# Early gate weights, one background list and early residuals in a one-core streaming-encoder layer

## Chip, cores and metric

The kernel runs on one core of a Trainium2 chip. The metric is the device time of one execution in microseconds: the median of three runs is 1506.96 us (1506.39 to 1509.68). The engines are named as in the profile: PE (TensorE, matrix products), DVE (VectorE), ACT (ScalarE), POOL (GpSimd) and SP (SyncE, which issues most loads).

## What is computed

One layer on 1024 tokens of width 1024, in float32. A first half mixes tokens in three branches, each with a sigmoid gate; a second half is a gated feed-forward network of width 2816.

```
n = rmsnorm(h);  proj = n @ w_in            # pool input, q, k, v, xq, 3 x 1024 gate columns
y_pool = pool_mixer(pool input) @ w_pool_o  # trailing means over 2, 4, 8, 16 tokens, 4 groups
y_sb   = stick_breaking(q, k, v) @ w_sb_o   # 8 heads, strictly causal
y_x    = cross_attention(xq, mem) @ w_x_o   # 4 heads, 256 memory tokens, softmax
merged = sum of sigmoid(gate_b) * y_b
h = h + rmsnorm(merged @ w_out)
gu = rmsnorm(h) @ w_ffn_in
h = h + rmsnorm((silu(gu[:, :2816]) * gu[:, 2816:]) @ w_ffn_out)
```

## The kernel before

**Products.** Tiles are 128 rows by 512 columns (C). Each float32 product is three fp32r matmuls (`mm3`, L167 to L171): every operand is split into a rounded part and the rest. A weight tile is loaded into `ws` (3 buffers) or `b2` (8 buffers), ACT casts it to `wh` and DVE subtracts to `wl` (5 buffers each; `split`, L163 and L164, for `ws`; `parts`, L250 and L251, for any tile). PSUM has eight banks: `pa` 3, `pz` 2, `pt` 2, `pv` 1.

**Strassen-like pairs.** Most projections go by `pairs` (L444): for two weight columns, four quarters of the weights (`quarters`, loads into four `b2` tiles) and seven products of half depth, of 4 x 3 matmuls of 512 columns each, instead of eight. The first two of the seven are `opening` (L434): bank `X` holds product 11, bank `Y` product 12, and L440 adds the copy of the first to the second. Then come S1 and S2, whose weights are differences made on DVE (L456, L460), then S4, S3 and 22. The activations' sums for S1 to S4 are made and split on DVE and ACT too (L516 to L537). The next job's opening is put between S3 and 22 of this one; the first call opens two jobs at its start.

**The order of the first half.** Pooling products and norms; products of the memory tokens; then three early gate tiles of branch 1 for the first half of the tokens (`early`, L510, weights by `split`), with the operand sums; then the first `pairs` call (xq, q 0, q 2), the keys (k 0, k 2), the values (seven products written out, L700 to L770), four gate pairs (branch 0, m = 0, 2, 4, 6), and the attention. The remaining gate tiles of branches 1 and 2 are the list `later` (L804): single products of 12 matmuls, which `fill(n)` puts between the attention's units.

**Background.** Small steps run at the `aside()` places: three in each job of `pairs`, one behind each of the first six products of the values. Sixteen are units of the cross-attention (`recall`, L624: scores L584 and L585, softmax L586 to L597, four transposes L604, products L615 and L616); they are put on the list after the first `pairs` call. They read `xq` back from DRAM, and SP issues these reads in program order. What is left after the values runs in a loop (L771). Then `w_mix` is split, and eight pooling steps (`pooled`, L646) and the first `fetch` of the attention's operands go on the list for the gate pairs.

**Attention.** `units` are 32 (head pair, pair of 128-token rows, head). `sticks` (L833) makes scores, sigmoids and running products on PE, ACT, POOL and DVE one unit ahead; `values` (L872) transposes (L881), splits on ACT and DVE (L174, L175) and multiplies with v (L893, L896). Before each unit's values stand as many fillers as its share of the work, four before the first, eight kept for the end.

**The end.** After the two halves of the merged product and the feed-forward network, the last product (22) is made tile by tile, four tiles of 128 rows; behind each, `finish` (L1265) loads the two residual halves (`load`, L115, on SP), squares (L1276), multiplies with the gain (L1279), takes the power on POOL (L180), multiplies and adds the residual (L1285) and writes half on SP and half on ACT (L1286). `load` keeps SP's order as the program is written; for the rest a scheduler sets each engine's order ahead of time from the program's order and a simulated time line.

Of the kernel before, what the change touches and what calls it, by code (L numbers as in the profile page):

```python
# [9 lines left out]
F32R = mybir.dt.float32r  # L10
# [4 lines left out]
P = 128  # L15
# [13 lines left out]
LEAD = 8  # L29
HOLD = 3  # L30
EARLY = 3
FILL_FIRST = 4
FILL_LAST = 8
TB = C // P
# [4 lines left out]
def hybrid_block(  # L39
# [77 lines left out]
    def ps_a():  # L117
        return pa.tile([P, C], F32, tag="pa", name="pa")
# [160 lines left out]
    for c in range(NC):  # L279
        rb = t_r()[:, :C]  # L280
        rms_rows(ssum[c], C, pc[:, c * TB : (c + 1) * TB], rb)
        rbc.append(rb)
        pool_step(4 + c)
        if c == 1:
            first_mk = [split(w_mk[0, half]) for half in range(2)]
        else:
            for q in range(HK):
                a11.append(normed_x(q, 0, t_c()[:, :C]))
                A["11"][q] = parts(a11[q], t_act(), t_act())
# [141 lines left out]
            load(raw[h][i], src[m + i, h])  # L431
        return raw

    def opening(raw, sink):  # L434
        (b11, b12), (b21, b22) = raw
        X, Y = ps_a(), ps_a()
        product(X, w_parts(b11), "11", True)
        p1 = copied(X)
        product(Y, w_parts(b21), "12", True)
        nc.vector.tensor_add(p1, Y, p1)  # L440
        sink(0, 0, p1)
        return X

    def pairs(jobs, raws=None):  # L444
# [1 line left out]
        raws = raws or [jobs[0][0]()]  # L446
        ahead = len(raws)

        opened = [opening(raws[j], jobs[j][1]) for j in range(ahead)]
        for j, (_, sink) in enumerate(jobs):  # L450
            (b11, b12), (b21, b22) = raws[j]
            if len(raws) == j + 1 < len(jobs):
# [56 lines left out]

    def early(m):  # L510
        for half in range(2):
            gate_step(KT + m, half, 0, split(w_gate[KT + m, half]))


    early(0)
# [130 lines left out]
    def pooled(g, c):  # L646
# [38 lines left out]
                nc.gpsimd.dma_start(d, t)  # L685
        return step

    pairs(
        [(lambda: quarters(w_xq, 0), to_parts(xq_d, 0))]
        + [(lambda m=m: quarters(w_q, m), to_parts(q_d, m)) for m in (0, 2)],  # L690
        xq_raws,
    )
    background += [recall(n) for n in range(len(units))]
    pairs([(lambda m=m: quarters(w_k, m), to_parts(k_d, m)) for m in (0, 2)])


    v_d = [
        [dram.tile([P, C], F32R, name=f"v{j}{h}") for h in range(2)] for j in range(KT)
    ]
    v_sb = [[None, None] for _ in range(KT)]  # L700
    W = C // 2
    raw = [[[None, None], [None, None]], [[None, None], [None, None]]]
    for h, i in ((0, 0), (1, 0), (0, 1), (1, 1)):
# [64 lines left out]
    sub2(b21, b21, b11)  # L768
    v_product(X, two(b21), "22")
    to_values(1, 0, X)  # L770
    while background:  # L771
        aside()


    heads = {}

    def fetch(p, c):

        if c == 0:
            heads[p] = [[[None] * NC for _ in range(2)] for _ in range(3)]  # L780
        qst, kh, kl = heads[p]
        for e in range(2):
            for tiles in (qst, kh, kl):
                tiles[e][c] = t_c(F32R)[:, :C]
            stacked(qst[e][c], q_d[p][c], e)
            twice(kl[e][c], k_d[p][c][1], e)
            twice(kh[e][c], k_d[p][c][0], e)
        if p % 2 == 0 and c == 1:
            for j in range(KT - 1, -1, -1):
                v = v_sb[j][p // 2] = t_a(F32R)  # L790
                load(v, v_d[j][p // 2])

    mix_h, mix_l = split(w_mix)
    background += [pooled(g, c) for g in range(4) for c in (1, 0)] + [lambda: fetch(0, 0)]
    pairs([(lambda m=m: quarters(w_gate, m), to_gate(0, m)) for m in range(0, KT, 2)])
    for q in range(HK):
        u = normed_x(q, 1, t_d()[:, :C])
        A["21"][q] = parts(u, t_act(), t_act())
# [4 lines left out]

    later = [  # L804
        (b * KT + m, half, c)
        for b in (1, 2)
        for m in range(KT)
        for half in range(2)
        for c in range(1 if b == 1 and m < EARLY else 0, NC)
    ]  # L810
# [451 lines left out]
        g_post[1][h] = t_r()[:, :C]  # L1262
        load(g_post[1][h], post[1:2, h * C : (h + 1) * C].broadcast_to([P, C]))

    def finish(t, first_ps):  # L1265

        st = small.tile([P, 8], F32, tag="st1", name="st1")
        res = []
        for h in range(2):
            u = t_b2()  # L1270
            load(u, hid_d[t][h])
            res.append(u)
        for h in (1, 0):
            src = first_ps if h == 0 and first_ps is not None else y[t][h]
            sq = t_d()[:, :C]
            nc.scalar.activation(sq, src, AF.Square, scale=1.0 / 32, accum_out=st[:, h : h + 1])  # L1276
            if src is not y[t][h]:
                y[t][h] = t_c()[:, :C]
            nc.vector.tensor_mul(y[t][h], src, g_post[1][h])  # L1279
        v = small.tile([P, 4], F32, tag="rv", name="rv")  # L1280
        nc.vector.tensor_scalar(v[:, 0:1], st[:, 0:1], st[:, 1:2], EPS, ALU.add, ALU.add)  # L1281
        r = inv_root(v, 1)
        for h in range(2):
            o = y[t][h]
            nc.vector.scalar_tensor_tensor(o, o, r[:, 0:1], res[h], ALU.mult, ALU.add)  # L1285
            (nc.gpsimd if t < TB else (nc.sync, nc.scalar)[h]).dma_start(  # L1286
                out[t, :, h * C : (h + 1) * C], o
            )
# [4 lines left out]
    for k in range(HF):  # L1293
# [2 lines left out]
        room = [t_act() if k < 8 else t_a(F32R) for _ in range(4)]  # L1296
        last.append((parts(u, *room[:2]), parts(b_of("T4", k), *room[2:])))
        if k < TB:
            finish(k, None)
    for i in range(TB):  # L1300
        add_bank(s5[i], X[i])
        y[TB + i][1] = s5[i]
    for i in range(TB):
        bs = slice(i * P, (i + 1) * P)
        for k in range(HF):
            (ah, al), (wh, wl) = last[k]
            mm3(X[i], ah[:, bs], al[:, bs], wh, wl, False, k == HF - 1, True)
        finish(TB + i, X[i])


# [76 lines left out]
```

## Time and profile before

| | |
|---|---|
| median of three runs | 1506.96 us (1506.39 to 1509.68) |
| profiled execution | 1507.43 us |
| its span, first to last instruction | 1505.7 us |
| mean granted TensorE clock | 0.988 |
| busy: PE, DVE, ACT, POOL | 96%, 69%, 47%, 22% |
| early gates and first openings | 60 to 110 us |
| last cross-attention units | 257 to 274 us |
| gate pairs | from 274 us |
| attention | 410 to 640 us |
| last tile's end | 1491 to 1505.7 us |

A matmul counts as busy from its start to its modelled end, and the next one starts before that; so a busy PE may still lose time, and the granted clock has to be read beside it. The span leaves out 1.7 us of the profiled execution's time. The table's stages are the stretches of the program in the order above; the rows below give each its idle time, its clock and its waits.

### The profile page before, as it was taken

Reading aid. Unit: us, or ns where it says so; the run is one execution under the profiler, and the core shown is the slowest. Engines: PE = TensorE matmul, PEld = TensorE weight load, DVE = VectorE, ACT = ScalarE, POOL = GpSimd, SP = SyncE. Lnnn points to the kernel's source line nnn. Section 1 sums busy time; section 2 is a strip of 40 time slices with the busy share of each in tenths; the row PEclk is TensorE's granted clock in tenths of the full one; section 3 lists DMA queues with packets and bytes.
Section 4 is the critical chain, followed back from the end, with each engine's and each line's share of the span. In section 5 each row is a group of like instructions: output and inputs, shape, how many; then the busy total and the mean of one; then the engine's idle time right before and its main releaser. Section 6 shows DMA issues by size and latency. Waiting matters only on the chain.

```text
span 1505.7 us, 20998 instructions
## 1 busy us (share of the span) xinstructions
PE 1449.7 (96%) x6914; PEld 1203.1 (80%) x6914; DVE 1037.0 (69%) x1732; ACT 706.1 (47%) x1405; POOL 330.6 (22%) x612
## 2 busy tenths in 40 slices
PE   9989999999999999899999999999999999999996
PEld 8768898777887888778887777888888887888875
DVE  8795777794879878745514597765566666478475
ACT  8554556553656656522235673233333333434452
POOL 0201212122244332354445310000011112000011
PEclk9999999999999999999999999999999999999998
DMA  8726446458322531475555454443465656754354
GB/s 277 221 96 183 140 127 189 151 184 274 109 96 84 164 122 59 147 232 187 154 161 193 145 180 152 152 130 127 140 195 191 195 175 212 233 184 147 108 151 161
DMA packets 126222, 245.77 MB, mean 163 GB/s; under 512 B 16656, under 2 KB 20256, under 8 KB 126112
## 3 DMA queue, kind: packets, MB, share of 16 engines
q1 hardware_dynamic: 97952, 173.09, 37.5%
q0 software_dynamic: 27584, 70.29, 13.4%
q8 instruction: 54, 0.88, 0.3%
q10 hardware_dynamic: 576, 1.05, 0.2%
q14 instruction: 56, 0.46, 0.1%
HBM read 174.11 MB, written 69.73 MB: 162 GB/s over the span
## 4 chain that ended last, share of the span: by engine, by line
PE 77%; DVE 7%; DMA 6%; issue 5%; ACT 2%; POOL 2%; SPq 1%; POOLq 0%; ACTq 0%; DVEq 0%
PE pa L169 16%; PE pa L170 15%; PE pa L171 15%; PE pz L171 5%; PE pz L170 5%; PE pz L169 5%; PE pt L171 3%; PE pt L169 3%; PE pt L170 3%; DMA ws<-in_w_gate_dram 2%; PE pt L881 1%; SPq L115 1%; DMA d<-in_x_dram 1%; PE pv L893 1%; PE pv L896 1%
## 5 line engine op out<-in xcount | busy, mean ns | idle before, releaser
L169 PE MATMUL pa<-act,wh 128*128 128x512 f32 (+1 forms) x572 | 226.5, 396 | 10.7 <-ACT wh L163 4.6
L171 PE MATMUL pa<-act,wl 128*128 128x512 f32 (+1 forms) x572 | 223.5, 394 | 1.3 <-DVE wl L251 1.3
L170 PE MATMUL pa<-act,wh 128*128 128x512 f32 (+1 forms) x572 | 224.1, 392 | 0.0
L250 ACT CAST wh<-b 128x512 fp32r<-128x512 f32 x159 | 97.9, 622 | 162.7 <-PE pa L170 100.2
L169 PEld LDWEIGHTS pa<-act,wh 128*128 128x128 f32 x572 | 109.1, 191 | 35.5 <-ACT wh L163 5.0
L251 DVE TENSOR_TENSOR wl<-b,wh 128x512 fp32r<-128x512 f32 x159 | 108.1, 685 | 36.4 <-ACT wh L250 23.6
L163 ACT CAST wh<-ws 128x512 fp32r<-128x512 f32 (+1 forms) x121 | 73.9, 612 | 120.0 <-PE pa L170 34.8
L171 PEld LDWEIGHTS pa<-act,wl 128*128 128x128 f32 x572 | 108.4, 190 | 24.2 <-DVE wl L251 2.2
L170 PEld LDWEIGHTS pa<-act,wh 128*128 128x128 f32 x572 | 109.2, 191 | 20.8
L250 ACT CAST wh<-ws 128x512 fp32r<-128x512 f32 x76 | 47.5, 625 | 105.9 <-DVE ws L1153 42.5
L164 POOL TENSOR_TENSOR wl<-ws,wh 128x512 fp32r<-128x512 f32 x52 | 67.8, 1311 | 78.0 <-ACT wh L163 78.0
L250 ACT CAST d<-b 128x512 fp32r<-128x512 f32 x66 | 40.7, 620 | 93.1 <-PE pt L170 46.0
L169 PE MATMUL pa<-a,wh 128*128 128x512 f32 x200 | 78.9, 397 | 4.0 <-ACT wh L250 1.7
L164 DVE TENSOR_TENSOR wl<-ws,wh 128x512 fp32r<-128x512 f32 (+1 forms) x69 | 46.1, 672 | 52.1 <-ACT wh L163 32.6
L251 DVE TENSOR_TENSOR d<-b,d 128x512 fp32r<-128x512 f32 x66 | 45.3, 689 | 52.8 <-ACT d L250 51.7
L171 PE MATMUL pa<-a,wl 128*128 128x512 f32 x200 | 78.2, 393 | 0.0
L170 PE MATMUL pa<-b,wh 128*128 128x512 f32 x196 | 76.5, 391 | 0.0
L175 DVE TENSOR_TENSOR d<-pt,d 128x512 fp32r<-128x512 f32 (+1 forms) x96 | 60.8, 637 | 16.7 <-ACT d L174 16.2
L1119 POOL DMA_DIRECT2D ff<-c x44 | 23.8, 540 | 215.2 <-DVE c L1174 123.6
L174 ACT CAST d<-pt 128x512 fp32r<-128x512 f32 (+1 forms) x96 | 52.7, 557 | 29.3 <-PE pt L881 15.1
L180 POOL TENSOR_TENSOR rc<-rv,mhalf 128x1 f32<-128x1 f32 (+2 forms) x15 | 14.3, 956 | 230.9 <-DVE rv L1281 199.0
L862 DVE TENSOR_TENSOR_SCAN r<-a,zero 128x512 f32<-128x512 f32 (+1 forms) x64 | 53.4, 842 | 15.4 <-POOL a L850 14.6
(419 smaller groups left out, 4043.0 us busy)
## 6 DMA issues: line engine op xcount, KB each, us to landing
b<-in_w_ffn_in_dram SPq DMA_DIRECT2D x88, 256.0 KB, 2.7
d<-gt SPq DMA_DIRECT2D x48, 256.0 KB, 2.9
ws<-in_w_ffn_in_dram SPq DMA_DIRECT2D x44, 256.0 KB, 2.8
ff<-c POOLq DMA_DIRECT2D x44, 256.0 KB, 3.1
b<-ffS SPq DMA_DIRECT2D x44, 256.0 KB, 2.6
ws<-in_w_gate_dram SPq DMA_DIRECT2D x38, 256.0 KB, 3.6
gt<-g POOLq DMA_DIRECT2D x36, 256.0 KB, 2.5
b<-ff SPq DMA_DIRECT2D x33, 256.0 KB, 3.6
```

The source lines that it names most:

```text
L115: tc.keep_in_program_order(queue.dma_start(dst, src))
L163: nc.scalar.copy(wh[:, :n], ws[:, :n])
L164: lo.tensor_sub(wl[:, :n], ws[:, :n], wh[:, :n].bitcast(F32))
L169: nc.tensor.matmul(ps, lh, rh, start=first, stop=False, skip_group_check=onto)
L170: nc.tensor.matmul(ps, lh, rl, start=False, stop=False, skip_group_check=onto)
L171: nc.tensor.matmul(ps, ll, rh, start=False, stop=last, skip_group_check=onto)
L174: nc.scalar.copy(hi, ps)
L175: nc.vector.tensor_sub(lo, ps, hi.bitcast(F32))
L250: nc.scalar.copy(hi, src)
L251: eng.tensor_sub(lo, src, hi.bitcast(F32))
L862: nc.vector.tensor_tensor_scan(ex[:, lo + 1 : C + 1], rest[:, lo:], zero.broadcast_to([P, C - lo]), start, ALU.mult, ALU.add,)
L1119: nc.gpsimd.dma_start(ff_d[n][k], t)
```

## The change

Five edits. The first gate tile's weights are loaded into the two `g` tiles while the first memory weights are loaded, and `early(0)` splits them from there. The second of the two openings of the first `pairs` call takes its `Y` from `pz`. The pairs of branch 0 cover m = 0 to 5 (`PAIRED`), and m = 6, 7 go to the head of `later`. All units of the cross-attention, the eight pooling steps and the first `fetch` are one list, filled when the weights of q 2 are loaded (at the second job of the first call); the loop that empties it stands behind the gate pairs, and `w_mix` is split before the first `pairs` call. In `finish` the loads of the residuals become `residual`, which for the last four tiles is called before the last product.

```
+PAIRED = 6
...
         if c == 1:
             first_mk = [split(w_mk[0, half]) for half in range(2)]
+            first_gate = [t_g(), t_g()]
+            for half in range(2):
+                load(first_gate[half], w_gate[KT, half])
...
-    def opening(raw, sink):
+    def opening(raw, sink, other=ps_a):
         (b11, b12), (b21, b22) = raw
-        X, Y = ps_a(), ps_a()
+        X, Y = ps_a(), other()
...
-        opened = [opening(raws[j], jobs[j][1]) for j in range(ahead)]
+        opened = [opening(raws[j], jobs[j][1], (ps_a, ps_z)[j]) for j in range(ahead)]
...
     def early(m):
         for half in range(2):
-            gate_step(KT + m, half, 0, split(w_gate[KT + m, half]))
+            w = w_parts(first_gate[half]) if m == 0 else split(w_gate[KT + m, half])
+            gate_step(KT + m, half, 0, w)
...
-    pairs(
-        [(lambda: quarters(w_xq, 0), to_parts(xq_d, 0))]
-        + [(lambda m=m: quarters(w_q, m), to_parts(q_d, m)) for m in (0, 2)],
-        xq_raws,
-    )
-    background += [recall(n) for n in range(len(units))]
...
+    mix_h, mix_l = split(w_mix)
...
+    def second_q():
+        background.extend(recall(n) for n in range(len(units)))
+        background.extend(pooled(g, c) for g in range(4) for c in (1, 0))
+        background.append(lambda: fetch(0, 0))
+        return quarters(w_q, 2)
+
+    pairs(
+        [
+            (None, to_parts(xq_d, 0)),
+            (None, to_parts(q_d, 0)),
+            (second_q, to_parts(q_d, 2)),
+        ],
+        xq_raws,
+    )
...
+    pairs([(lambda m=m: quarters(w_gate, m), to_gate(0, m)) for m in range(0, PAIRED, 2)])
     while background:
         aside()
...
-    mix_h, mix_l = split(w_mix)
-    background += [pooled(g, c) for g in range(4) for c in (1, 0)] + [lambda: fetch(0, 0)]
-    pairs([(lambda m=m: quarters(w_gate, m), to_gate(0, m)) for m in range(0, KT, 2)])
...
-        for b in (1, 2)
-        for m in range(KT)
+        for b in range(3)
+        for m in range(PAIRED if b == 0 else 0, KT)
...
+    def residual(t):
+        res = [t_b2(), t_b2()]
+        for h in range(2):
+            load(res[h], hid_d[t][h])
+        return res
+
+    def finish(t, first_ps, res):
...
+    res = [residual(TB + i) for i in range(TB)]
     for i in range(TB):
...
-        finish(TB + i, X[i])
+        finish(TB + i, X[i], res[i])
```

DVE's order around the first job's S2 is, before (a row is line, operation, output from inputs; `b_1039` to `b_1045` are the four weight quarters of xq; L440 is the addition of the second job's opening):

```order
L251 TENSOR_TENSOR a<-c,a 128x512
L251 TENSOR_TENSOR b_1200<-r,b_1199 128x512
L251 TENSOR_TENSOR d<-c,d 128x512
L460 TENSOR_TENSOR b_1039<-b_1045,b_1039 128x512
L471 TENSOR_TENSOR b_1041<-b_1041,b_1039 128x512
L440 TENSOR_TENSOR c<-pa,c 128x512
L251 TENSOR_TENSOR wl<-b_1039,wh 128x512
```

And now, where L440, L460 and L251 have become L444, L464 and L252:

```order
L444 TENSOR_TENSOR c<-pz,c 128x512
L252 TENSOR_TENSOR a<-c,a 128x512
L252 TENSOR_TENSOR b_1195<-d,b_1194 128x512
L471 TENSOR_TENSOR b_1091<-b_1093,b_1091 128x512
L252 TENSOR_TENSOR d<-c,d 128x512
L252 TENSOR_TENSOR a<-c,a 128x512
L464 TENSOR_TENSOR b_1039<-b_1045,b_1039 128x512
```

The second opening's addition, now from `pz`, has moved six operations ahead of the difference for S2; the difference itself stands one instruction later, counted from the engine's start.

PE's order between the values and the gate pairs is, before (L615 and L616 are the products of a cross-attention unit, L604 its transposes, L584 and L585 the scores of the next):

```order
L171 MATMUL pa<-act,wl 128x512
L615 MATMUL pv<-d,c 128x256
L616 MATMUL pv<-d,c 128x256
L615 MATMUL pv<-d,c 128x256
L616 MATMUL pv<-d,c 128x256
L604 MATMUL pt<-ident,c 128x128 x6
L584 MATMUL pz<-c,r 128x256
L585 MATMUL pz<-c,r 128x256
L604 MATMUL pt<-ident,c 128x128 x2
```

And now, behind the last product of the values (`mm3` is L170 to L172; products into `pv` are those of a pooling step):

```order
L170 MATMUL pa<-act,wh 128x512
L171 MATMUL pa<-act,wh 128x512
L170 MATMUL pv<-d,wh 128x512
L172 MATMUL pa<-act,wl 128x512
L171 MATMUL pv<-d,wh 128x512
L172 MATMUL pv<-d,wl 128x512
L170 MATMUL pa<-a,wh 128x512
L171 MATMUL pa<-a,wh 128x512
```

The cross-attention's small products have left this place, and gate products with a pooling step between them stand there.

PE's order at the end of the attention is, before (L881 transposes, L893 and L896 multiply with v):

```order
L881 MATMUL pt<-ident,b_7318 128x128
L881 MATMUL pt<-ident,b_7329 128x128
L881 MATMUL pt<-ident,b_7318 128x128
L893 MATMUL pv<-d,a 128x256
L896 MATMUL pv<-d,a 128x256
L893 MATMUL pv<-d,a 128x128
L896 MATMUL pv<-d,a 128x128
```

And now, with the products with v in L905 and L908:

```order
L170 MATMUL pa<-act,wh 128x512
L171 MATMUL pa<-act,wh 128x512
L172 MATMUL pa<-act,wl 128x512
L170 MATMUL pa<-act,wh 128x512
L905 MATMUL pv<-d,a 128x256
L908 MATMUL pv<-d,a 128x256
L905 MATMUL pv<-d,a 128x128
L908 MATMUL pv<-d,a 128x128
```

Gate products have moved between the transposes and the products with v of one of the last units.

## Rows read from the trace of the kernel before

**Rows 1.** The page, part 1: busy us (share of the span) xinstructions of each engine.

```profile
PE 1449.7 (96%) x6914; PEld 1203.1 (80%) x6914; DVE 1037.0 (69%) x1732; ACT 706.1 (47%) x1405; POOL 330.6 (22%) x612
```

**Rows 2.** Stretches: from:to, length; busy us by engine; PE clock, DMA share, GB/s.

```profile
60.00:80.00 20.00, 15.40 (x86) 13.34 (x85) 18.11 (x34) 9.57 (x19) 4.70 (x9) 0.91 1.02 315
80.00:110.00 30.00, 25.20 (x102) 19.52 (x101) 29.96 (x51) 16.55 (x30) 2.70 (x5) 0.94 0.14 43
257.00:274.00 17.00, 12.81 (x55) 10.15 (x55) 13.20 (x37) 9.24 (x26) 2.21 (x5) 0.80 0.46 133
274.00:344.00 70.00, 69.45 (x300) 56.43 (x300) 61.56 (x113) 37.55 (x65) 16.66 (x31) 0.98 0.57 181
410.00:640.00 230.00, 217.76 (x1217) 184.61 (x1215) 187.52 (x294) 140.85 (x317) 81.79 (x217) 0.98 0.36 114
620.00:640.00 20.00, 15.97 (x100) 13.55 (x98) 15.53 (x30) 13.02 (x32) 7.87 (x17) 0.90 0.59 197
655.00:820.00 165.00, 165.00 (x726) 135.80 (x725) 73.13 (x99) 48.21 (x96) 84.51 (x73) 1.00 0.54 169
```

**Rows 3.** Time lines of the end: start us, us, engine, instruction, [idle before <-releaser].

```profile
1491.27 0.39 PE L171 MATMUL pv<-a 128*128 128x512 f32 x1
...
1484.05 0.60 ACT L1276 ACTIVATE d<-pa 128x512 f32<-128x512 f32 x1 [8.24 <-PE pa L171]
...
1491.69 0.60 ACT L1276 ACTIVATE d<-pv 128x512 f32<-128x512 f32 x1 [3.00 <-PE pv L171]
...
1477.52 0.68 DVE L251 TENSOR_TENSOR a<-a 128x512 fp32r<-128x512 f32 x1
...
1486.82 1.41 DVE L1285 SCALAR_TENSOR_TENSOR c<-c,rc,b 128x512 f32<-128x512 f32 x2
...
1500.66 0.75 DVE L1285 SCALAR_TENSOR_TENSOR c<-c,rc,b 128x512 f32<-128x512 f32 x1 [3.21 <-DMA b<-hid]
1501.90 0.75 DVE L1285 SCALAR_TENSOR_TENSOR c<-c,rc,b 128x512 f32<-128x512 f32 x1 [0.49 <-DMA b<-hid]
...
1497.24 0.87 SPq L115 DMA_DIRECT2D b<-hid  x2
```

**Rows 4.** Waits of PE, 250 to 276 us: line, releaser: us, times, longest.

```profile
PE pv L615 <- DVE d L175: 1.9, 1, 1.9
...
PE pa L169 <- ACT c L417: 0.3, 1, 0.3
```

**Rows 5.** Waits of PE, whole span: the one on the read of `xq`.

```profile
PE pz L584 <- DMA r<-xq: 0.8, 1, 0.8
```

**Rows 6.** Time line of SP's queue, 46 to 190 us.

```profile
57.11 2.42 SPq L115 DMA_DIRECT2D ws<-in_w_gate_dram  x2
59.57 3.09 SPq L115 DMA_DIRECT2D d<-in_x_dram  x6
...
141.49 38.78 SPq L115 DMA_DIRECT2D r<-xq  x8
```

**Rows 7.** Waits of PE, 46 to 112 us.

```profile
PE pa L169 <- ACT wh L163: 4.6, 1, 4.6
PE pa L169 <- DVE c L440: 2.9, 1, 2.9
PE pa L169 <- ACT wh L250: 1.7, 1, 1.7
```

**Rows 8.** Time line of DVE, 60 to 106 us.

```profile
60.60 0.42 DVE L384 TENSOR_TENSOR t<-pa,c 128x256 f32<-128x256 f32 x1 [0.26 <-PE pa L171]
...
65.43 1.62 DVE L256 SCALAR_TENSOR_TENSOR d<-d,g_sb,r 128x512 f32<-128x512 f32 x2 [1.26 <-DMA d<-in_x_dram]
...
105.34 0.68 DVE L460 TENSOR_TENSOR b<-b,b 128x512 f32<-128x512 f32 x1
```

**Rows 9.** The page, part 5: busy us, mean ns, idle before, of weight casts and subtractions.

```profile
L250 ACT CAST wh<-b 128x512 fp32r<-128x512 f32 x159 | 97.9, 622 | 162.7 <-PE pa L170 100.2
...
L251 DVE TENSOR_TENSOR wl<-b,wh 128x512 fp32r<-128x512 f32 x159 | 108.1, 685 | 36.4 <-ACT wh L250 23.6
```

More of the change, by code (lines that the diff above doesn't have):

```diff
@@ L686, in pooled, with fetch @@
         return step
-    pairs(
-        [(lambda: quarters(w_xq, 0), to_parts(xq_d, 0))]
-        + [(lambda m=m: quarters(w_q, m), to_parts(q_d, m)) for m in (0, 2)],
-        xq_raws,
-    )
-    background += [recall(n) for n in range(len(units))]
-    pairs([(lambda m=m: quarters(w_k, m), to_parts(k_d, m)) for m in (0, 2)])
+    heads = {}
+    def fetch(p, c):
+        if c == 0:
+            heads[p] = [[[None] * NC for _ in range(2)] for _ in range(3)]
+        qst, kh, kl = heads[p]
+        for e in range(2):
+            for tiles in (qst, kh, kl):
+                tiles[e][c] = t_c(F32R)[:, :C]
+            stacked(qst[e][c], q_d[p][c], e)
+            twice(kl[e][c], k_d[p][c][1], e)
+            twice(kh[e][c], k_d[p][c][0], e)
+        if p % 2 == 0 and c == 1:
+            for j in range(KT - 1, -1, -1):
+                v = v_sb[j][p // 2] = t_a(F32R)
+                load(v, v_d[j][p // 2])
+    mix_h, mix_l = split(w_mix)
+    v_sb = [[None, None] for _ in range(KT)]
     v_d = [
@@ L699, in hybrid_block @@
     ]
-    v_sb = [[None, None] for _ in range(KT)]
+    def second_q():
[11 more added lines that the diff above has]
+    )
+    pairs([(lambda m=m: quarters(w_k, m), to_parts(k_d, m)) for m in (0, 2)])
     W = C // 2
@@ L770, in hybrid_block @@
     to_values(1, 0, X)
+    pairs([(lambda m=m: quarters(w_gate, m), to_gate(0, m)) for m in range(0, PAIRED, 2)])
     while background:
         aside()
[L775 to L791, printed above, removed]
-    mix_h, mix_l = split(w_mix)
-    background += [pooled(g, c) for g in range(4) for c in (1, 0)] + [lambda: fetch(0, 0)]
-    pairs([(lambda m=m: quarters(w_gate, m), to_gate(0, m)) for m in range(0, KT, 2)])
     for q in range(HK):
@@ L1263, in hybrid_block @@
         load(g_post[1][h], post[1:2, h * C : (h + 1) * C].broadcast_to([P, C]))
-    def finish(t, first_ps):
-        st = small.tile([P, 8], F32, tag="st1", name="st1")
[L1268 to L1272, printed above, removed]
+    def residual(t):
[4 more added lines that the diff above has]
+    def finish(t, first_ps, res):
+        st = small.tile([P, 8], F32, tag="st1", name="st1")
         for h in (1, 0):
@@ L1298, in hybrid_block @@
         if k < TB:
-            finish(k, None)
+            finish(k, None, residual(k))
     for i in range(TB):
```

## The prediction

> **What bounds the kernel now.** I read the page's engine lines first. TensorE (PE) has work in flight for 96% of the span and VectorE (DVE) for 69% [rows 1], so I look for time that PE does not use, and then for what else is late there. Busy time flatters PE, since a matmul of 512 columns is in flight for 0.39 us but the next one starts sooner: in the dense stretch from 655 to 820 us 726 matmuls take 165.00 us, 0.2273 us each [rows 2]. That is my price for one matmul of 512 columns. Half a clock also counts as busy, so I read the granted clock beside it: it is one of two levels, 1.2 or 2.4 GHz, and a mean of 0.80 over 17 us means 3.4 us less of full clock.
>
> The table by stage then shows where PE is not fed. From 60 to 110 us (early gates, first openings) PE is idle for 9.4 us and the clock gives away 0.09 of 20 and 0.06 of 30 us, 3.6 us more. From 257 to 274 us (the last four cross-attention units, with hardly any product beside them) the clock is 0.80. In the attention, 410 to 640 us, 12.2 us are idle and 0.02 of 230 us, 4.6 us, is lost to the clock; the last 20 us of it hold 4.0 us idle and 2.0 us of clock. From 655 us on nothing is lost for long. At the end, PE's last matmul starts at 1491.27 us and the span ends at 1505.7 us [rows 2, 3].
>
> **The change part by part.**
>
> Two gate tiles leave the Strassen-like pairs for the attention's fillers. A pair is 7 products of 12 matmuls, 84; the same two tiles done directly are 2 tiles x 2 halves x 2 column blocks x 12 = 96. So 84 x 0.2273 = 19.1 us leave the gate stage, which is dense (274 to 344 us: PE 69.45 of 70, [rows 2]), and 21.8 us come into the attention. Net work: 12 x 0.2273 = **+2.7 us**.
>
> What these 96 matmuls bring is cover. The attention's unused time is a ceiling of 12.2 + 4.6 = 16.8 us; the floor is nothing, if the extra products land where PE was fed already. The order decides. Before, the fillers are used up before the last units: transposes and value products follow each other directly, and 4.0 + 2.0 us of the last 20 are lost. After, groups of 7 to 14 filler matmuls stand ahead of the values of the last units, and the last two units have merge products between them. I take those 6 us nearly whole and a third of the other 11: **-10 us**, with ends 0 and -17. Two gaps without filler stand in the new order too, in the middle of the attention, as before. DVE is busy for 187.52 of 230 us there [rows 2], and the fillers add only four weight splits to it, so it does not become the bound.
>
> The background list. Sixteen cross-attention units (`recall`), eight pooling units and one fetch are now drained one at each `aside`. There are 27 of these places (3 in each of two first jobs from the third weight load on, 6 in the keys, 6 in the values, 9 in three gate pairs) for 25 steps, so none is left over. Before, four units were left after the values and ran with nothing beside them. What they cost: 6.1 us of waits between 250 and 276 us, in six rows from 1.9 down to 0.3 [rows 4], 3.4 us of clock from 257 to 274 and 0.02 x 70 = 1.4 us after it [rows 2], together 10.9 us. What may come back: the first unit needs a round trip through DRAM, which cost 0.8 us before [rows 5] and may cost 0 to 2 now; the key weights stand on SP's queue behind the reads of `xq`, which block it for long (38.78 us for eight of them before, [rows 6]), but some 70 matmuls of 512 columns, 16 us, lie between the scores that free that queue and the first key product, against some 4 us for the loads; and two pooling units ride in the values. I take **-9 us**, with ends -3 and -11. The gate stage keeps DVE below PE: it had 61.56 us of DVE in 70 for four pairs and eight pooling units, and now has three and six in 252 x 0.2273 + 18 x 0.2273 = 61.4 us of PE.
>
> The early load of the first gate weights, and the second opening's bank in `pz` instead of `pa`. The waits that they aim at are plain: 4.6 us for weights that landed late, 2.9 us for a `pa` bank that the addition in L440 frees, and 1.7 us for the weights of S2 [rows 7]. With 3.6 us of clock that is 13 us. But I do not count them, because another row is late next: DVE is busy for 29.96 of the 30 us from 80 to 110 us [rows 2], working through the operand sums and splits in its own order, and PE's S2 cannot start before L460, at 105.34 us in that row of operations [rows 8]. From 60.60 us to there DVE idles for 1.26 us only [rows 8], so 43.5 us are work; the new order has the same operations and puts L460 one operation (0.6 us) later. The x loads that DVE waited for (the 1.26 us) are issued behind the gate weights at 57.11 us, and some 2.4 to 4 us sooner without them [rows 6]. So L460 moves from 105.34 to between 104.4 and 106 us, and the stalls only change their place: **-0.5 us**. Ends: -3.5, if PE also finds something to do meanwhile and the half clock goes, and +2, if one longer idle time before S2 lets the clock fall, as 60 to 80 us shows (0.91, 1.8 us).
>
> The Trainium skill has a rule that speaks for this reading: TensorE: Matmul & The Clock Gate, section Architectural detail, says that the queues of ScalarE and VectorE are strictly first in, first out. By it no weight split can overtake the sums queued ahead of it on DVE. The trace agrees: the addition that frees the bank runs at its place among back-to-back operations, although PE waits. Were DVE free to choose, all 13 us would go and the sum would be 12 us lower.
>
> The residuals of the last four tiles are loaded before the last product. At the end SP issues an output, then the two residual loads of the next tile, and the output must wait for its result: so each pair of loads is issued only after the tile before is done (1497.24 us for the last) and DVE waits for them, 3.21 us before its last but one operation [rows 3]. Loaded early, the end is PE's last matmul (in flight until 1491.66) plus one tile's own chain. In the first of the four tiles that chain, which waited for no residual, takes 2.77 us from the start of its square to its two last operations (1484.05 to 1486.82), and these take 1.41; the last square starts at 1491.69 [rows 3]. 1491.69 + 2.77 + 1.41 = 1495.9 us against 1501.90 + 0.75 = 1502.65. **-6.8 us**, with ends -6 and -8. SP has no output ahead of the eight loads now, and the buffers that they need are free when DVE's last splits end, 9 us before the first tile's last operations (1477.52 + 0.68 against 1486.82, [rows 3]).
>
> **The rivals.** First, the cover is not used: the fillers run where PE was fed, so the attention pays all 96 matmuls, and only 3 us of the recalls' waits go. +2.7 - 3 - 0.5 - 6.8 = -7.6 gives 1499. For it speaks that the attention's stalls are chains through ScalarE, GpSimd and DVE, with DVE at 82%; against it the order at the end. That the early residuals don't come early, since they need all eight `b2` buffers, would put the time at about 1490 alone.
>
> Second, everything goes: the attention's whole 17 us or the opening's 13 us, which gives 1483 - 7 or 1483 - 12, 1471 to 1476, and below with both. The wall on DVE speaks against the second.
>
> Third, slower: the split of `w_mix` now stands before the first pairs and holds one of the five `wh` and `wl` buffers through queries, keys and values, where it did so in the gate stage alone. If products there could no longer be split ahead, each would show a cast and a subtraction, 0.62 + 0.69 = 1.3 us [rows 9]; 21 + 14 + 7 = 42 products make 55 us, so 1483 + 55 = 1538. It decides from 24 / 42 = 0.57 us a product on. Against it: the gate stage of the kernel before ran with four buffers and PE was busy for 69.45 of 70 us [rows 2].
>
> **How the numbers follow.** +2.7 - 10 - 9 - 0.5 - 6.8 = -23.6. The profiled execution took 1507.43 us, 1.7 more than its span and 0.5 more than the median of the three runs; 1507.43 - 23.6 = 1483.8, and 1483.3 beside the median of 1506.96. Forecast with its own range, 1474 to 1491: 65 in 100. Cover not used, 1491 to 1504: 18. Everything goes, below 1474: 10. Gains just eaten up, 1504 to 1510: 3. Starved weights, above 1510: 4. The range is 1470 to 1499: it leaves out some 6 above it of the first neighbour's 18, 3 below it of the second's 10, and the last 7. A measurement of this kernel tells some 0.2%, 3 us, from no change: faster 0.93, same 0.03, slower 0.04.
>
> **What would show it.** Right: no L584, L604 or L615 waits between values and gates and a clock near 1.00 there; fewer idle microseconds in the attention's last 20, although it is longer; PE still idle for 5 us or more ahead of S2 between 90 and 107 us, with DVE back to back; the last DVE operation some 4 us after PE's last matmul. Wrong: PE idle in the attention grows, waits on `wh` or `wl` in the values, PE waiting for key or value weights behind SP's reads of `xq`, or S2 clearly before 103 us.

## The result

The changed kernel takes 1491.76 us (median of four runs, 1489.89 to 1494.19) beside 1507.95 us for the kernel before (four runs): ratio 0.9893, 95% interval 0.9878 to 0.9907, which is 16.2 us less. The forecast was 23.6 us less, 1483, with a range of 1470 to 1499: the time lies in the range, and 7.4 of the 23.6 us did not come. The profiled execution has a span of 1491.3 us, 14.4 less than before.

The page of the changed kernel, part 1 (busy us, share of the span, instructions), beside [rows 1]:

```profile
PE 1446.5 (97%) x6926; PEld 1201.3 (81%) x6926; DVE 1032.1 (69%) x1722; ACT 702.0 (47%) x1399; POOL 333.6 (22%) x612
```

PE has the twelve matmuls more that the sum began with. The stretches that answer to [rows 2], and the two in which something new appears (from:to, length, busy us by engine, then granted clock, DMA share, GB/s):

```profile
60.00:80.00 20.00, 16.54 (x90) 14.23 (x89) 17.40 (x33) 9.17 (x18) 4.72 (x9) 0.91 0.86 271
80.00:110.00 30.00, 25.96 (x99) 20.13 (x98) 30.00 (x51) 17.71 (x33) 3.23 (x6) 0.85 0.16 52
264.00:270.00 6.00, 1.23 (x3) 0.48 (x3) 2.89 (x5) 2.25 (x5) 2.73 (x6) 0.87 1.10 329
270.00:276.00 6.00, 5.95 (x15) 4.69 (x16) 1.34 (x3) 1.61 (x4) 1.66 (x4) 0.56 0.97 314
...
619.00:639.00 20.00, 20.00 (x104) 16.89 (x103) 6.00 (x12) 6.20 (x13) 8.64 (x12) 1.00 0.62 189
```

The last 20 us of the attention are now full at full clock (15.97 us and 0.90 before). But a hole has opened at 264 us, just where the four leftover units had been: PE works for 1.23 of 6 us, and then at little more than half clock for 6 more.

To say where the 14.4 us came from, I take from the trace the time between the starts of neighbouring matmuls and subtract what that pair of shapes takes in the kernel before where nothing interrupts it (0.2273 us for two of 512 columns). What is left is time lost, to idling and to half clock alike. The attention counts here from its first scores (343 us before), so it holds more than the stretch from 410 us on in which the forecast saw its 16.8 us. By stage, in us:

| stage | forecast | lost before | lost after | difference |
|---|---|---|---|---|
| start to first S2 | openings -0.5 | 17.6 | 16.2 | -1.4 |
| first S2 to values | list, | 1.8 | 5.2 | +3.4 |
| values | with both neighbours | 2.5 | 1.4 | -1.0 |
| values to first attention scores | -9 | 14.1 | 11.3 | -2.8 |
| attention | cover -10 | 35.4 | 25.6 | -9.8 |
| later products | | 19.6 | 19.4 | -0.2 |
| last matmul to end | -6.8 | 14.5 | 9.1 | -5.3 |
| work, 12 matmuls | +2.7 | | | +2.7 |

Two terms came as forecast, the tail gave 1.5 us less, and the list, worth 9 in the forecast, shows 0.4 in this account. The experiments are about that.

The runs were measured in four series, on different chips, and the kernel before had medians of 1507.95 to 1511.48 us in them; so a run is compared by its ratio to the kernel before in its own series; 0.001 is 1.5 us, and the intervals reach about 0.002, 3 us, to either side.

### The profile page after: what moved, and what is told of

It reads as the page before. It is cut to its first block, busy times and chain, and to the rows that moved or that the text cites. A ratio compares the mean times of both kernels' runs of the same rounds, so it can differ in the third digit from the quotient of the medians.

```text
span 1491.3 us, 21003 instructions
## 1 busy us (share of the span) xinstructions
PE 1446.5 (97%) x6926; PEld 1201.3 (81%) x6926; DVE 1032.1 (69%) x1722; ACT 702.0 (47%) x1399; POOL 333.6 (22%) x612
## 4 chain that ended last, share of the span: by engine, by line
PE 84%; DVE 6%; issue 4%; DMA 3%; ACT 2%; POOL 1%; SPq 0%; POOLq 0%; DVEq 0%; ACTq 0%
PE pa L170 17%; PE pa L172 17%; PE pa L171 17%; PE pz L172 5%; PE pz L171 5%; PE pz L170 5%; PE pt L172 3%; PE pt L170 3%; PE pt L171 3%; PE pt L893 2%; PE pv L908 1%; PE pv L905 1%; PE pv L171 1%; PE pv L170 1%; PE pv L172 1%
## 5 line engine op out<-in xcount | busy, mean ns | idle before, releaser
L170 PE MATMUL pa<-act,wh 128*128 128x512 f32 (+1 forms) x584 | 230.6, 395 | 10.8 <-ACT wh L164 3.5
L172 PE MATMUL pa<-act,wl 128*128 128x512 f32 (+1 forms) x584 | 229.8, 396 | 3.9 <-DVE wl L252 3.8
L171 PE MATMUL pa<-act,wh 128*128 128x512 f32 (+1 forms) x584 | 230.0, 394 | 0.0
L251 ACT CAST wh<-b 128x512 fp32r<-128x512 f32 x152 | 93.5, 621 | 146.4 <-PE pa L171 86.3
L170 PEld LDWEIGHTS pa<-act,wh 128*128 128x128 f32 x584 | 111.3, 191 | 34.8 <-issue 4.1
L172 PEld LDWEIGHTS pa<-act,wl 128*128 128x128 f32 x584 | 111.4, 191 | 27.0 <-DVE wl L252 5.2
L171 PEld LDWEIGHTS pa<-act,wh 128*128 128x128 f32 x584 | 111.1, 190 | 20.9
L252 DVE TENSOR_TENSOR wl<-b,wh 128x512 fp32r<-128x512 f32 x152 | 103.2, 685 | 30.7 <-ACT wh L251 26.0
L164 ACT CAST wh<-ws 128x512 fp32r<-128x512 f32 (+1 forms) x119 | 72.7, 612 | 104.4 <-PE pa L171 34.2
L251 ACT CAST wh<-ws 128x512 fp32r<-128x512 f32 x80 | 49.9, 625 | 106.6 <-DVE ws L1165 42.1
L251 ACT CAST d<-b 128x512 fp32r<-128x512 f32 x66 | 40.7, 620 | 90.6 <-PE pt L171 45.8
L252 DVE TENSOR_TENSOR d<-b,d 128x512 fp32r<-128x512 f32 x66 | 45.3, 689 | 51.0 <-ACT d L251 50.9
L170 PE MATMUL pa<-a,wh 128*128 128x512 f32 x192 | 75.9, 398 | 2.6 <-ACT wh L251 1.2
L172 PE MATMUL pa<-a,wl 128*128 128x512 f32 x192 | 74.6, 392 | 0.0
L252 DVE TENSOR_TENSOR wl<-ws,wh 128x512 fp32r<-128x512 f32 x80 | 54.9, 688 | 17.8 <-ACT wh L251 15.4
L181 POOL TENSOR_TENSOR rc<-rv,mhalf 128x1 f32<-128x1 f32 (+2 forms) x15 | 14.5, 969 | 229.8 <-DVE rv L1294 198.3
```

What stands on the lines that cost most here:

```text
L164: nc.scalar.copy(wh[:, :n], ws[:, :n])
L170: nc.tensor.matmul(ps, lh, rh, start=first, stop=False, skip_group_check=onto)
L171: nc.tensor.matmul(ps, lh, rl, start=False, stop=False, skip_group_check=onto)
L172: nc.tensor.matmul(ps, ll, rh, start=False, stop=last, skip_group_check=onto)
L251: nc.scalar.copy(hi, src)
L252: eng.tensor_sub(lo, src, hi.bitcast(F32))
```

## The hole at 264 us

Waits of PE in the changed kernel, 250 to 280 us (line, releaser: us, times, longest); these stand where the six waits of [rows 4] were:

```profile
PE pa L170 <- DVE d L359: 3.5, 1, 3.5
PE pv L170 <- ACT d L251: 1.0, 1, 1.0
PE pv L171 <- DVE d L252: 0.4, 1, 0.4
```

L359 is the value split that empties the `pa` bank which the first gate pair needs. What it waited for stands in the waits of ACT in the same stretch, which casts the high halves ahead of it:

```profile
ACT d L358 <- DMA v<-d: 2.3, 2, 1.3
ACT d L685 <- DMA v<-d: 2.3, 1, 2.3
...
ACT d L251 <- DMA xo<-d: 1.7, 1, 1.7
```

All three write a `d` tile and wait until a store from an older one has landed. There are six such tiles; a pooling step (L685 is one) takes four, a quarter of the values four, the end of a cross-attention head pair four. Two pooling steps now run among the values. But the DMA engines are also full there (share 1.10, 329 GB/s), so the stores might be late for that reason alone.

**e1**, the value splits in other tiles:

```
     t = t_d(F32R)[:, :C]
+    if b < 3:
+        t = wpool.tile([P, C], F32R, tag="ws", name="ws", bufs=3)
```

> The changed kernel, with three of the four value splits of each quarter written into ws tiles instead of d tiles; nothing else. Theory 'buffers': in the changed kernel two pooling steps now run among the values; each needs four of the six d tiles, each quarter of the values needs four too, and a d tile comes free only when its store has landed. So the last value splits are late, the gate pair's first product waits for their bank (3.5 us for L359 at 266.6 us, 4.9 us in three waits) and the clock halves after it (0.56 over 270 to 276 us, 2.6 us). Then here the wait for L359 falls below 1 us, the clock there stays above 0.9, and the time falls from 1491.8 by 4 to 8 us, to 1484 to 1488. Theory 'transfers': the stores land late because the 16 DMA engines are full (share 1.10 from 264 to 270 us) whatever the tiles are; then the wait stays at 3 us or more and the time between 1490 and 1494.

Measured: 1488.54 us, ratio 0.9842 (0.9818 to 0.9866), against 0.9893 and, in another series (e5), 0.9904 for the changed kernel. The stretches and the waits of PE of e1, same columns as above:

```profile
264.00:270.00 6.00, 5.50 (x25) 4.18 (x24) 3.92 (x8) 3.56 (x7) 0.81 (x3) 1.00 1.06 323
270.00:276.00 6.00, 6.00 (x28) 4.97 (x27) 5.97 (x14) 2.98 (x6) 2.07 (x4) 1.00 0.63 188
```

```profile
PE pa L170 <- ACT c L421: 0.5, 1, 0.5
```

The DMA engines are as full as in the changed kernel (1.06, 323 GB/s) and the hole is gone; the clock stays at 1.00. So it was the tiles. Lost time between values and attention falls from 11.3 to 2.9 us, 8.4, and the ratios differ by 0.005 to 0.006, some 8 us.

**e2**, no pooling among the values: the eight steps and the fetch go on the list behind them.

```
     def second_q():
         background.extend(recall(n) for n in range(len(units)))
-        background.extend(pooled(g, c) for g in range(4) for c in (1, 0))
-        background.append(lambda: fetch(0, 0))
         return quarters(w_q, 2)
...
+    background.extend(pooled(g, c) for g in range(4) for c in (1, 0))
+    background.append(lambda: fetch(0, 0))
     pairs([(lambda m=m: quarters(w_gate, m), to_gate(0, m)) for m in range(0, PAIRED, 2)])
```

> The changed kernel, with the eight pooling steps and the first fetch put on the list behind the values, so that they run in the nine places of the three gate pairs, and the cross-attention units alone before. Theory 'buffers': the 8 us around 264 to 276 us go, but two more pooling steps, some 6 us of VectorE each, come into a gate stage of 55 us in which VectorE is already the busier one from 276 to 310 us (31.4 of 34 us); I expect 1486 to 1491. Theory 'transfers': the wait ahead of the first gate pair stays, and the two steps cost beside it: 1492 to 1497.

Measured: 1494.81 us, ratio 0.9886 (0.9862 to 0.9910), level with the changed kernel. The time lies where 'transfers' had it, but the wait for L359, on which that theory rests, falls to 1.1 us, and another takes its place. PE's waits in e2, 320 to 345 us:

```profile
PE pa L170 <- ACT wh L251: 7.8, 1, 7.8
PE pv L170 <- ACT d L251: 0.7, 1, 0.7
```

That is the cast of the attention's first filler weights, behind the last gate pair. Neither theory had it, and it leads to the fillers.

## The fillers and the list

**e9**, the kernel before with nothing but the two gate tiles moved:

```
-    pairs([(lambda m=m: quarters(w_gate, m), to_gate(0, m)) for m in range(0, KT, 2)])
+    pairs([(lambda m=m: quarters(w_gate, m), to_gate(0, m)) for m in range(0, 6, 2)])
...
-        for b in (1, 2)
-        for m in range(KT)
+        for b in range(3)
+        for m in range(6 if b == 0 else 0, KT)
```

> The kernel before, with only the two gate tiles moved from the pairs to the fillers. The prediction's step: 7.3 us faster than before (cover 10, work 2.7), ratio 0.995. Theory 'joint', after e3 and e7, which were level: the attention's idle and half clock fall by some 8 us as forecast, but the gate stage, now three pairs for the same eight pooling steps, ends with PE waiting 7 to 9 us for the fillers' first weights, so the ratio is 0.999 to 1.004.

Measured: 1513.58 us, ratio 1.0021 (1.0006 to 1.0035): alone, the move brings nothing and rather costs, 1 to 5 us. PE's waits in e9, 335 to 356 us, and SP's queue there (start us, us, instruction):

```profile
PE pa L169 <- ACT wh L250: 8.9, 1, 8.9
...
336.36 2.20 SPq L115 DMA_DIRECT2D d<-in_x_dram  x4
338.61 10.18 SPq L115 DMA_DIRECT2D ws<-in_w_gate_dram  x5
```

The fillers' weights are loaded by SP behind four loads of x, and these go into `d` tiles, which the last pooling steps hold: SP waits 2.7 us there for their stores (334 to 338 us). PE has nothing else between the last pair and the first filler. The place in the queue is not the whole of the 8.9 us: from 338.6 to 346.0 us the 16 DMA engines have a share of 0.94, and the five weight loads there take 6.3 us from issue to landing (median), where that kernel's page has 3.3 for all of them. In the kernel before the same two groups were issued later still:

```profile
342.50 2.10 SPq L115 DMA_DIRECT2D d<-in_x_dram  x4
344.65 10.57 SPq L115 DMA_DIRECT2D ws<-in_w_gate_dram  x6
```

but a fourth pair was running until then, and no wait of PE from 335 to 356 us was over 0.8 us. The fourth pair had been the cover of that queue. The lost time of e9's attention stage is 34.0 us, 8.9 of it this wait; the other 25.1 beside 35.4 before are the cover that the forecast had put at 10.

**e3 and e7**, the list as before, with six and with eight gate tiles in pairs; the diff of e3 against the changed kernel:

```
-    mix_h, mix_l = split(w_mix)
...
-        background.extend(recall(n) for n in range(len(units)))
-        background.extend(pooled(g, c) for g in range(4) for c in (1, 0))
-        background.append(lambda: fetch(0, 0))
...
+    background += [recall(n) for n in range(len(units))]
     pairs([(lambda m=m: quarters(w_k, m), to_parts(k_d, m)) for m in (0, 2)])
...
+    while background:
+        aside()
+    mix_h, mix_l = split(w_mix)
+    background += [pooled(g, c) for g in range(4) for c in (1, 0)] + [lambda: fetch(0, 0)]
     pairs([(lambda m=m: quarters(w_gate, m), to_gate(0, m)) for m in range(0, PAIRED, 2)])
-    while background:
-        aside()
```

> The changed kernel, with the background list as before: cross-attention units from the keys on, the loop that empties the list behind the values, then w_mix, pooling steps and fetch for the gate pairs. The prediction's step: the one list is worth 9 us, so 1500.8 here. The account of the two traces by stage (idle and half clock from the first S2 to the attention's first scores: 18.4 us before, 18.0 after): it is worth 0.4 us, so 1490 to 1494, with waits for L584, L604 and L615 behind the values in place of the wait for L359.

> The list as before and all eight tiles in pairs: of the change only the early gate weights, the bank in pz and the early residuals are left. If the list and the fillers each brought their own sum whatever the other does, this would be the list's run plus 7.3 us, some 1512 beside 1505 for e3. Theory 'joint': the wait of 8.1 us for the fillers' weights is gone, and this is faster than e3 by 2 to 6 us: 1499 to 1503.

**e6 and e5**, the changed kernel with eight tiles in pairs, and as it is; e7 and e12 have the same line:

```
-PAIRED = 6
+PAIRED = 8
```

> The changed kernel with all eight gate tiles of branch 0 in pairs, as before (PAIRED = 8); the one list then has 30 places for its 25 steps. The prediction's step: cover less work, 10 - 2.7 = 7.3 us, so that much above the changed kernel, 1499. Theory 'joint': in the run with the list as before PE waits 8.1 us at the end of the gate stage, because the fillers' first weights stand on SP's queue behind x loads that wait for d tiles of the last pooling steps. So the two tiles fewer in pairs cost something there that only the one list hides. With the one list, eight tiles in pairs leave no such wait (under 1 us for filler weights around the first scores of the attention), and the attention has the idle time of the kernel before: 3 to 8 us above the changed kernel.

> The changed kernel once more, so that the three runs beside it, and those of e1 to e4 by their ratios, have it as their measure on the same chip: 1490 to 1496.

| ratio to the kernel before | list as before | one list |
|---|---|---|
| eight tiles in pairs | e7, 1502.09 us: 0.9953 (0.9934 to 0.9971) | e6, 1493.33 us: 0.9898 (0.9876 to 0.9920) |
| six tiles in pairs | e3, 1505.05 us: 0.9955 (0.9939 to 0.9971) | e5, 1495.93 us: 0.9904 (0.9883 to 0.9924) |

The columns differ by 0.0055 and 0.0051: the one list is worth some 8 us with either number of pairs. The account by stage had put it at 0.4, and fell: it compared the new list over three pairs with the old list over four, and set against the list what the shorter gate stage costs. The rows are level: the move of the two tiles brings nothing that these runs can tell, with either list. Both forecasts for e6, 3 to 8 us above the changed kernel, fell with that (no wait for filler weights, the other half of 'joint', held). e7's 1502.09 us lie in the 1499 to 1503 expected, but its ratio is that of e3, so it is not shown to be faster. With the old list e3 shows the filler weights' wait of e9 (8.1 us). With the new one the pooling steps end earlier and 2.4 us of it are left, in e5 from 325 to 340 us:

```profile
PE pa L170 <- ACT wh L251: 2.4, 1, 2.4
PE pa L170 <- DVE c L473: 0.8, 1, 0.8
```

And e6, whose attention runs out of fillers as the kernel before did, has its loss at the same place, its last 20 us:

```profile
617.00:637.00 20.00, 15.91 (x86) 12.93 (x86) 12.71 (x27) 11.10 (x28) 11.59 (x20) 0.91 0.68 217
```

e5 loses 27.8 us in the attention and e6 33.6, so the cover is there, 5.8 us in this pair of profiles; 2.7 of work and some 1.5 between values and attention are paid for it. The rest goes behind the attention. PE's waits in e5, 600 to 670 and 1430 to 1480 us:

```profile
PE pa L170 <- ACT wh L164: 1.3, 1, 1.3
PE pa L172 <- POOL wl L165: 0.6, 1, 0.6
...
PE pa L170 <- DVE c L1256: 2.2, 1, 2.2
```

The first two are for weights of the merged product, and e6 has neither; of the third it has 0.3 us. That one is 1.0 us in the changed kernel's first profile and 0.3 in e1, so it may be chance. With these waits the span of e5's profile is 1493.3 us and that of e6's 1491.6.

## The openings and the tail

**e8**, the changed kernel with first gate weights and openings as before:

```
-            first_gate = [t_g(), t_g()]
-            for half in range(2):
-                load(first_gate[half], w_gate[KT, half])
...
-        opened = [opening(raws[j], jobs[j][1], (ps_a, ps_z)[j]) for j in range(ahead)]
+        opened = [opening(raws[j], jobs[j][1]) for j in range(ahead)]
...
-            w = w_parts(first_gate[half]) if m == 0 else split(w_gate[KT + m, half])
+            w = split(w_gate[KT + m, half])
```

> The changed kernel without the early load of the first gate weights and with both openings in pa. The prediction's step: 0.5 us (from a loss of 2 to a gain of 3.5), VectorE's row of operations being late next, so 1490 to 1495, L464 within 1.5 us of its time in the changed kernel. The rival of the prediction, that all of 13 us go, would put it at 1503 or more. The account by stage (idle and half clock ahead of the first S2: 17.6 us before, 11.3 to 16.2 in five runs with the new opening) allows 1.4 to 6 us.

Measured: 1501.89 us, ratio 0.9949 (0.9928 to 0.9970) against e5's 0.9904: some 7 us, with 4 either way, and above the 1490 to 1495 that was expected. (e7, in which of the whole change only openings and tail are left, bounds it from the other side: 7.1 us below the kernel before, of which the tail is 5.3.) The difference for S2, on which the forecast's wall rested, starts here (changed kernel, e5, e8; before: 105.34, [rows 8]):

```profile
106.34 0.68 DVE L464 TENSOR_TENSOR b<-b,b 128x512 f32<-128x512 f32 x1
```

```profile
104.14 0.70 DVE L464 TENSOR_TENSOR b<-b,b 128x512 f32<-128x512 f32 x1
```

```profile
105.95 0.70 DVE L461 TENSOR_TENSOR b<-b,b 128x512 f32<-128x512 f32 x1
```

So DVE's row of operations moved by little more than 1 us from 105.34, about as forecast. The Trainium skill's rule (TensorE: Matmul & The Clock Gate, Architectural detail), that DVE's queue is strictly first in, first out, goes with the three rows, but does not follow from them.

What PE does ahead of this wall changed, and the forecast did not look at it. PE's first matmuls of S1 and of S2 in e5, then in e8:

```profile
97.17 0.47 PE L170 MATMUL pa<-act,wh 128*128 128x512 f32 x1 [1.75 <-DVE c L444]
105.95 0.50 PE L170 MATMUL pa<-a,wh 128*128 128x512 f32 x1 [1.24 <-ACT wh L251]
```

```profile
107.40 0.47 PE L170 MATMUL pa<-act,wh 128*128 128x512 f32 x1 [2.10 <-ACT wh L251]
111.81 0.40 PE L170 MATMUL pa<-a,wh 128*128 128x512 f32 x1
```

With both openings in `pa`, S1 starts only when the second opening's addition, which stands behind the wall (106.55 us in e8, 106.66 before), has freed a bank; the profile puts the end of the wait in e8 down to a cast that ends within 0.2 us of it. With `pz`, the twelve matmuls of S1, 2.7 us, come ahead of the wall. The first matmul of S3, which has the same work ahead of it in all kernels to within four matmuls, starts at 115.7 us before and 117.3 in e8, at 115.3 in the changed kernel's first profile and at 111.3 to 113.7 in e1, e2, e4, e5 and e6, which have the same openings. The clock differs too. 60 to 80 and 80 to 112 us, e5 first and then e8:

```profile
60.00:80.00 20.00, 18.68 (x105) 15.75 (x104) 19.87 (x37) 12.40 (x25) 4.73 (x9) 1.00 0.86 281
80.00:112.00 32.00, 26.70 (x104) 20.05 (x104) 30.64 (x52) 16.29 (x29) 3.23 (x6) 0.89 0.26 83
```

```profile
60.00:80.00 20.00, 14.92 (x82) 12.74 (x81) 17.73 (x33) 9.55 (x19) 4.71 (x9) 0.84 1.03 327
80.00:112.00 32.00, 27.24 (x102) 21.19 (x101) 30.26 (x51) 16.46 (x31) 3.23 (x6) 0.88 0.17 53
```

e8 loses 0.16 x 20 + 0.12 x 32 = 7.0 us of full clock, e5 3.5. With the early load PE has products where it idled 5 us, and the half clock of that place goes. But it is no gain over the kernel before, which with 0.91 from 60 to 80 us [rows 2] and

```profile
80.00:112.00 32.00, 27.20 (x111) 21.17 (x110) 31.35 (x53) 17.66 (x32) 3.23 (x6) 0.95 0.19 60
```

lost 1.8 + 1.6 = 3.4 us. The changed kernel's first profile lost 0.09 x 20 + 0.16 x 32 = 6.9 us (S2 at 108.1 us): it waited 3.5 us for the weights of a later early gate; the same wait is 0.5 us in e5 and 0.6 in e1.

**e10**, `w_mix` split when the list is filled and not before the first pairs:

```
-    mix_h, mix_l = split(w_mix)
+    mix_h = mix_l = None
...
     def second_q():
+        nonlocal mix_h, mix_l
+        mix_h, mix_l = split(w_mix)
```

> The changed kernel, with w_mix loaded and split when the background list is filled and not before the first pairs call. In the runs that split it early and have the new openings the first S2 starts between 105.3 and 106.2 us (108.1 in the changed kernel's first profile), in e3 and e7, which split it behind the values, at 103.3 and 103.9. If holding one wh and wl tile and its place on VectorE through the openings is what costs these 2 us, S2 starts by 104.2 us here and the ratio is 0.988 to 0.989 against 0.990. If not, S2 is at 105 or later and the time level.

Measured: 1499.62 us, ratio 0.9924 (0.9907 to 0.9942), not the 0.988 to 0.989 expected and rather slower than e5, though the intervals overlap. S2 starts at 104.1 us, 1.9 sooner than in e5, so the early split does cost that; but the time lost from S2 to the values is 9.8 us instead of 4.4. The split has to stand somewhere, and in this place it costs more.

**e4**, the residuals as before:

```
-    res = [residual(TB + i) for i in range(TB)]
...
-        finish(TB + i, X[i], res[i])
+        finish(TB + i, X[i], residual(TB + i))
```

> The changed kernel, with the residuals of the last four tiles loaded inside finish as before. The prediction's step: 6.8 us, so 1498.6. The account of the two traces (from PE's last matmul to the end of the span 14.5 us before, 9.1 after): 5.3 us, so 1497.1.

Measured: 1499.31 us, ratio 0.9915 (0.9890 to 0.9941), 2 to 3 us above the changed kernel with 5 either way. The trace measures this better than the runs: from the last matmul to the end 14.8 us in e4 and e9, 14.5 in the kernel before, and 9.1 to 9.5 in the eleven other profiles. The end of the changed kernel beside [rows 3]: ACT's last square, DVE's last operations, SP's outputs.

```profile
1482.61 0.60 ACT L1289 ACTIVATE d<-pv 128x512 f32<-128x512 f32 x1 [3.01 <-PE pv L172]
...
1485.69 1.41 DVE L1298 SCALAR_TENSOR_TENSOR c<-c,rc,b 128x512 f32<-128x512 f32 x2 [0.72 <-POOL rc L181]
...
1478.51 8.29 SPq L1299 DMA_DIRECT2D out_dram<-c  x4
```

No wait on `hid` is left. The chain from square to last operations takes 3.08 us where the sum had 2.77; and from the end of DVE's work to the end of the span it is 4.2 us (1487.1 to 1491.3) where it had been 3.0 (1502.65 to 1505.7).

## The three repairs together

**e11** joins e1, e10 and the first three filler weight loads ahead of the four x loads; **e12** is the same with `PAIRED = 8`.

```
     for _ in range(3):
         gate_load()
+    for q in range(HK):
+        u = normed_x(q, 1, t_d()[:, :C])
+        A["21"][q] = parts(u, t_act(), t_act())
```

The same three lines are taken out ahead of `later`.

> The changed kernel with three things: value splits through ws tiles (e1), w_mix late (e10), and the first three loads of the fillers' gate weights ahead of the four x loads that wait for d tiles. By 'buffers' and 'joint': e1's 0.9842, less 2 us for w_mix and 1 to 3 us for the end of the gate stage, ratio 0.981 to 0.983. If the 8 us in e1 were a matter of that order alone, 0.985 to 0.990.

> As e11, with all eight gate tiles in pairs. If the fillers pay for themselves once the waits at the gate stage are gone, as the prediction's step says, this is 3 to 7 us slower than e11. If e5 and e6, which were level, tell the whole of it, level again within 2 us.

Measured: e11 1486.0 us, ratio 0.9828 (0.9809 to 0.9848), the lowest here, with an interval that overlaps with e1's; e12 1488.5 us, 0.9854 (0.9837 to 0.9872). No wait for filler weights is left in e11 (the longest from 310 to 330 us is 1.0), and now the two tiles among the fillers seem to bring 2 to 4 us, with intervals that overlap; expected were 3 to 7, or none. e11 contains the late `w_mix`, which e10 shows to be no gain by itself; without it e11 might be faster still, which was not run.

## Why the forecast held, point by point

The time lies in the range, but the range is 29 us wide: 1491.76 is just outside the 1474 to 1491 that the forecast called its own, in the band that it kept for unused cover, and the cover was used. So the mechanisms were right in part, and the number owes something to the width. Where the missing 7.4 us went can be told in two ways. By the runs, openings and tail together bring 7.1 us (e7; forecast 7.3) and the list 8 (forecast 9), while the fillers, cover and work together, bring nothing that shows (e5 against e6, e3 against e7; forecast 7.3). By the account of stages the fillers' cover came and the list's stages are short by 8 us, the size of the hole that e1 removes. The second way charges the list with what the shorter gate stage costs, so the first is the better account: the list came near its size, with a hole in it that could be mended, and the fillers' gain was paid back elsewhere.

- **Work, +2.7.** As forecast: twelve matmuls.
- **Cover in the attention, -10.** As forecast in its place: 9.8 us in the changed kernel, 10.3 in e9. The step that failed is the one before it, "so 19.1 us leave the gate stage, which is dense": it priced the gate pairs as work that leaves, and did not ask what they covered. They covered the queue of loads for the first fillers. Alone that costs 8.9 us (e9), in the changed kernel 1.2 to 2.4. The weights of the merged product behind the attention were not asked for either.
- **The background list, -9.** Undone, it costs 8 us (e3 against e5, e7 against e6), so the size was right; the reason was half of it. The leftover units' waits went. In their place came the `d` tiles' hole, 8 us (e1), against which stands that pooling, done earlier, no longer holds up the fillers' weights. The 3.4 us more between S2 and values can't be laid to the list: e3 and e7, with the list as before, lose some 6 us there, and the cause stays open. "Two pooling units ride in the values" was named in the prediction and costed at nothing beside its wide end; the pool that they share with the values was not looked at. In the account of stages the hole is what the sum lacks.
- **Early gate weights and bank, -0.5 (-3.5 to +2).** The wall on DVE stands at 103.5 to 104.8 us in five profiles of unchanged openings and w_mix (e1, e2, e4, e5, e6) and at 106.3 in the changed kernel's first, against a forecast of 104.4 to 106. Of the 13 us of waits and clock most stayed (PE idles 9.4 us from 60 to 112 us before, 7.5 in the changed kernel and 6.6 in e5), so that rival fell. But that the stalls only change their place was too strict: its far end, "if PE also finds something to do meanwhile", came in part, as the twelve matmuls of S1 ahead of the wall. The half clock did not go: 3.4 us before, 3.5 in e5, 6.9 in the changed kernel's first profile. The account has 1.4 us for this stage, the start of S3 0.4 in that profile and 2.0 to 4.4 in the five others, and e8's ratio allows more.
- **Residuals, -6.8 (-6 to -8).** -5.3: mechanism right, the size off by 0.3 us in the chain and 1.2 us in the last outputs, whose time the sum had taken as unchanged.
- **The third rival, starved weights.** It did not happen as such (no product waits on `wh` in the values for over 1 us), but `w_mix` early delays S2 by 2 us (e5 against e3, e7, e10).

The parts undone one by one add up to more than the whole: 8 for the list, 7 for the openings, 5.3 for the tail, against 16.2. The intervals of the first two are 4 us wide to either side, and each part's worth depends on the others, as e9 shows for the fillers. Of the forecast's own signs, no L584, L604 or L615 wait, the full last 20 us and the last DVE operation some 4 us behind PE came true; the clock near 1.00 between values and gates did not (0.87 and 0.56), and PE idled only 2.9 us from 90 to 107 us where 5 were expected (5.2 in e5).

## What to carry to other kernels

Work that is moved away from a dense stage takes its cover along: list what waits behind that stage (here loads queued behind loads that wait for tiles) and ask what will be running in the time that it needs. When two streams of background work are joined in one list, count the tiles of each pool that both hold until their stores have landed, not the engines' time alone. When a fixed operation of another engine holds up a product, ask which other products a free bank would let run ahead of it. A wait that shows between two engines is often decided two steps back, by a tile and a store; giving one stream tiles that lie idle there (e1) is a cheaper try than moving it (e2).

## What the runs showed of the hardware that was not expected

A wait of 4.9 us in three pieces was followed by 6 us at a granted clock of 0.56, nearly all at 1.2 of 2.4 GHz, so that the hole cost half as much again as its idle time; in e1, with no gap of over 0.5 us there, the clock stayed at 1.00. And 16 DMA engines at a share of 1.06 with 323 GB/s did not delay PE in e1, though the same stretch looked like a shortage of bandwidth.
